# Expert stage of a hybrid trunk layer: TensorE in source order, gathers and scatters in few groups

## The chip, the cores and the metric

One NeuronCore of one Trainium2 chip runs the whole program. The metric is the time of one execution on the device, in microseconds. The kernel is written with a planner (Tile): the program text gives instructions and data dependences; the planner allots buffers, sets semaphores and, by its own simulated time, chooses the order in which each engine issues. All operands are float32 in HBM.

## The reference, cut to what matters

One layer on 512 latent and 256 context tokens of width 2048: modulation, one input projection, two mixers (S5 and DeltaNet), output projection and LayerNorm; then an expert-choice mixture of experts on the 512 latent tokens, gate and a second LayerNorm. The change touches only the mixture and what follows it:

```python
aff = softmax(h @ router_w); gate, idx = top_k(aff.swapaxes(1, 2), cap)   # 16 experts, cap = 64 tokens each
sel = h[idx]                                                              # (16, 64, 2048)
hid = silu(sel @ w1) * (sel @ w3)                                         # w1, w3: 2048 x 1024 for each expert
y = (hid @ w2) * gate                                                     # w2: 1024 x 2048 for each expert
ff = zeros.at[idx].add(y)
x = layer_norm(ALPHA * x + g2 * ff, ln2_g, ln2_b)
```

## The kernel before, in words

The expert stage (lines 1845 to 1876) takes the experts two at a time, eight pairs `pr`. The 64 tokens of one expert fill one half of TensorE's columns, those of the other the other half (`tile_position=(0, 64 * a)`, a = 0, 1). A matmul with f32 operands shows as two records in the profile.

For each pair the work is:

- `gather` (L1444): VectorE writes a one-hot matrix `oh` (L1450); TensorE multiplies the 512 token rows `K.y` (names in the profile: mixed) with it, 16 matmuls or 32 records for each of four groups q (L1458); ScalarE applies the modulation while it copies a group from PSUM to `selT` (L1461). `oh` and `selT` have one buffer each.
- `expert_in` (L1508): eight steps of four loads of 1 MB (`load_in`, the DMA issue is L1477), each step 16 matmuls (32 records, L1522) into four PSUM banks `acc4`. Then `hid` is made (ScalarE L1527, VectorE L1528 and L1529), transposed (L1534) and copied to `hT` (L1535). `slots` (L1492) transposes `oh` into the scatter matrix `G` and fetches the gates `gc`.
- `expert_out` (L1545): two halves of the output columns, four steps each, a step being two loads of 1 MB and 8 matmuls (16 records, L1556). After each half `gated` (L1599) multiplies by gate and `g2r` (L1604), and splits the result in two parts `yp` (L1605, L1606). After steps 1 to 7 and at the end, a function `fill` inserts other work: a gather group of the next pair at even steps, scatter blocks 0 and 1 at steps 6 and 7.
- `scatter_chunk` (L1610): for one block of 512 columns, four times two matmuls (L1616) into a bank of `pp`, and VectorE adds it to `acc` (L1618). Blocks 2 and 3 come during the next pair's `expert_in`.

`merge` interleaves two generators in the text; but the text is only a priority, and the planner may reorder TensorE's instructions as its simulation finds data ready. DMA issues are all on SyncE's queue, in order. The loads go through 13 rotating buffers `ws` of 1 MB (`NWS`) and seven once-used ones `wy` for the first pair; a load waits until TensorE has read what was in its buffer.

PSUM has four banks `mp`, three banks `pp` (gather, scatter, transposes) and one `po`. In SBUF `hid`, `yp` and `ln1g` share two buffers (tag row), `ln1b` and `g2r` share one (tag g2r).

`acc_start` (L1638) makes the residual: rows of ln1 are spread over the partitions by `on_rows` (four transposes to a bank, then a copy by ScalarE, L1634 and L1635), VectorE multiplies (L1649) and GpSimd adds (L1650), eight operations of 128x1024 each; then `g2r` is made by `on_rows`. It is called once, between the first pair's `expert_in` and its `expert_out`. The last pair has its own second product `expert_last` (L1566), which ends in `K.fin` (L1593), and `finish` (L1655) normalises and stores.

Of the kernel before, what the change touches and what calls it, by code (L numbers as in the profile page):

```python
# [11 lines left out]
F32 = mybir.dt.float32  # L12
# [7 lines left out]
MUL, ADD, SUB = ALU.mult, ALU.add, ALU.subtract  # L20
# [6 lines left out]
KT = D // 128  # L27
# [18 lines left out]
def bc(a, shape):  # L46
    return a.to_broadcast(shape)


def mp(K, shape=(128, 4, 128), tag="mp"):  # L50
    return K.ps.tile(list(shape), F32, name=tag, tag=tag, bufs=K.banks[tag])


def pp(K, n=512):
    t = K.ps.tile([128, 512], F32, name="pp", tag="pp", bufs=K.banks["pp"])
    return t[:, :n]
# [796 lines left out]
def merge(*parts):  # L853

    live = [[g, n, 0] for g, n in parts]
    while live:
        e = min(live, key=lambda x: x[2] / x[1])
        e[2] += 1
        try:
            next(e[0])  # L860
        except StopIteration:
            live.remove(e)
# [6 lines left out]
GA = 1  # L869
# [574 lines left out]
def gather(K, pr, ep, S):  # L1444

    nc = K.nc
    V, A, T = nc.vector, nc.scalar, nc.tensor
    oh = ep.tile([128, 4, 2, 64], F32, name="oh")
    for a in range(2):
        V.tensor_tensor(oh[:, :, a], bc(K.iota64[:, None, :], [128, 4, 64]), bc(K.slot[:, :, 2 * pr + a:2 * pr + a + 1], [128, 4, 64]), op=ALU.is_equal)  # L1450
    S.oh = ohf = oh.rearrange("p b a s -> p b (a s)")
    S.selT = ep.tile([128, KT, 128], F32, name="selT")
    for q in range(4):
        pg = pp(K).rearrange("p (a b) -> p a b", a=4)
        for j in range(4):
            k = 4 * q + j
            for b in range(4):
                T.matmul(pg[:, j], K.y[:, k, b], ohf[:, b], start=(b == 0), stop=(b == 3))  # L1458
        for j in range(4):
            k = 4 * q + j  # L1460
            A.activation(S.selT[:, k], pg[:, j], AF.Identity, scale=K.A[:, k:k + 1], bias=K.B[:, k:k + 1])  # L1461
        yield
# [18 lines left out]
def load_in(K, I, pr, k0, w, a, gate=None):  # L1481
    return load(K, [128, 2, FF], ap(I[("exp_w1", "exp_w3")[w]], (2 * pr + a) * D * FF + k0 * 128 * FF, [[FF, 128], [128 * FF, 2], [1, FF]]), gate)
# [9 lines left out]
def slots(K, pr, S):  # L1492

    V, A, T = K.nc.vector, K.nc.scalar, K.nc.tensor
    S.G = K.ep2.tile([128, NL], F32R, name="G")
    pg = pp(K)
    for b in range(4):
        T.transpose(pg[:, 128 * b:128 * b + 128], S.oh[:, b], K.ident)
    A.copy(S.G, pg)
    pg = pp(K, 2)  # L1500
    for b in range(4):
        T.matmul(pg, S.oh[:, b], K.aff[:, b, 2 * pr:2 * pr + 2], start=(b == 0), stop=(b == 3))
    S.gc = K.ep2.tile([128, 1], F32, name="gc", bufs=2)
    for a in range(2):
        V.tensor_copy(S.gc[64 * a:64 * a + 64], pg[64 * a:64 * a + 64, a:a + 1])


def expert_in(K, I, pr, S):  # L1508
    nc = K.nc
    V, A, T = nc.vector, nc.scalar, nc.tensor  # L1510
    acc4 = [mp(K, (128, 512)) for _ in range(4)]
    for k0 in range(0, KT, 2):
        ws = {}
        for w in range(2):
            for a in range(2):
                ws[w, a] = load_in(K, I, pr, k0, w, a)
        for w in range(2):
            for kk in range(2):
                k = k0 + kk
                for c in range(2):  # L1520
                    for a in range(2):
                        T.matmul(acc4[2 * w + c][64 * a:64 * a + 64], S.selT[:, k, 64 * a:64 * a + 64], ws[w, a][:, kk, 512 * c:512 * c + 512],  # L1522
                                 start=(k == 0), stop=(k == KT - 1), tile_position=(0, 64 * a))
        yield
    hid = K.ep2.tile([128, 2, 512], F32, name="hid", tag="row", bufs=2)
    for c in range(2):
        A.activation(hid[:, c], acc4[c], AF.Tanh, scale=0.5)  # L1527
        V.scalar_tensor_tensor(hid[:, c], hid[:, c], 1.0, acc4[c], op0=ADD, op1=MUL)  # L1528
        V.scalar_tensor_tensor(hid[:, c], hid[:, c], 0.5, acc4[2 + c], op0=MUL, op1=MUL)  # L1529
    S.hT = K.ep2.tile([128, 8, 128], F32, name="hT")  # L1530
    for c in range(2):
        pt = pp(K).rearrange("p (a b) -> p a b", a=4)
        for j in range(4):
            T.transpose(pt[:, j], hid[:, c, 128 * j:128 * j + 128], K.ident)  # L1534
        A.copy(S.hT[:, 4 * c:4 * c + 4], pt)  # L1535
    slots(K, pr, S)
    yield


def load_out(K, I, pr, a, f, n, c0, w):  # L1540
# [69 lines left out]
def scatter_chunk(K, S, c, end=False):  # L1610
    s = slice(512 * c, 512 * c + 512)
    t = S.yp.pop(c)
    for b in range(4):
        ps = K.fin[b] if end else pp(K)
        for i in range(2):
            K.nc.tensor.matmul(ps, S.G[:, 128 * b:128 * b + 128], t[:, i], start=not end and i == 0, stop=i == 1)  # L1616
        if not end:
            K.nc.vector.tensor_tensor(K.acc[:, b, s], K.acc[:, b, s], ps, op=ADD)  # L1618
        if K.st2 is not None:
            K.nc.vector.bn_stats(K.st2[:, b, c], ps if end else K.acc[:, b, s])  # L1620


def scatter(K, S):
    for c in (2, 3):
        scatter_chunk(K, S, c)
        yield


def on_rows(K, dst, cols, scale=1.0, n=4):

    for q in range(n):
        pt = pp(K)
        for j in range(4):
            K.nc.tensor.transpose(pt[:, 128 * j:128 * j + 128], bc(cols[:, 4 * q + j:4 * q + j + 1], [128, 128]), K.ident)  # L1634
        K.nc.scalar.activation(dst[:, 512 * q:512 * q + 512], pt, AF.Copy, scale=scale)  # L1635


def acc_start(K, I, pool):  # L1638

    nc = K.nc  # L1640
    K.acc = pool.tile([128, 4, D], F32, name="acc")
    lb = pool.tile([128, D], F32, name="ln1b", tag="g2r")
    on_rows(K, lb, K.cols[:, 112:128], ALPHA)
    for h in range(2):
        lg = pool.tile([128, 8, 128], F32, name="ln1g", tag="row", bufs=2)
        on_rows(K, lg.rearrange("p k c -> p (k c)"), K.cols[:, 96 + 8 * h:104 + 8 * h], ALPHA, 2)
        s = slice(1024 * h, 1024 * h + 1024)
        for b in range(4):
            nc.vector.tensor_tensor(K.acc[:, b, s].rearrange("p (k c) -> p k c", k=8), K.y[:, 8 * h:8 * h + 8, b], lg, op=MUL)  # L1649
            nc.gpsimd.tensor_tensor(K.acc[:, b, s], K.acc[:, b, s], lb[:, s], op=ADD)  # L1650
    K.g2r = pool.tile([128, D], F32, name="g2r", tag="g2r")
    on_rows(K, K.g2r, K.g2[:, :, 0])


def finish(K, I, O, ep, lg, lb):  # L1655
# [22 lines left out]
def hybrid_trunk_kernel(tc, I, O):  # L1678
    nc = tc.nc
    K = Ctx()  # L1680
    K.nc, K.tc = nc, tc
    with ExitStack() as es:
# [24 lines left out]
        right = lambda name: tc.tile_pool(name=name, bufs=1, side="right", reuse_waits="tile")  # L1707
# [125 lines left out]
        with tc.tile_pool(name="p3", bufs=1, reuse_waits="tile") as p3:  # L1833
# [8 lines left out]
            wy = ExitStack()  # L1842
            K.wy = wy.enter_context(right("wy"))
            route(K, plog, p3)
        with tc.tile_pool(name="ep", bufs=1, reuse_waits="tile") as ep, ExitStack() as e2s:
            K.st2 = None
            S = [Ctx() for _ in range(8)]
            first = gather(K, 0, ep, S[0])
            for _ in range(GA):
                next(first)  # L1850
            begun = expert_in(K, I, 0, S[0])
            merge((first, 4 - GA), (itertools.islice(begun, 8), 8))
            wy.close()
            K.ep2 = e2s.enter_context(right("ep2"))
            for _ in begun:
                pass
            acc_start(K, I, K.ep2)
            for pr in range(8):
                S[pr].yp = {}
                if pr:  # L1860
                    merge((expert_in(K, I, pr, S[pr]), 9), (scatter(K, S[pr - 1]), 3))
                if pr < 7:
                    nxt = gather(K, pr + 1, ep, S[pr + 1])

                    def fill(step):
                        if step % 2 == 0:
                            next(nxt, None)
                        if step in (6, 7):
                            scatter_chunk(K, S[pr], step - 6)
                    expert_out(K, I, pr, S[pr], fill)  # L1870
            K.st2 = ep.tile([128, 4, 4, 6], F32, name="st2")
            l2 = K.yh("ln2", F32).rearrange("p (a q) n -> p a (q n)", a=4)
            l2 = [l2[:, i] for i in range(2)]
            for i in range(2):
                on_rows(K, l2[i], K.ln2[:, i])
            expert_last(K, I, 7, S[7])
            finish(K, I, O, ep, *l2)


# [26 lines left out]
```

## Time and profile before

| | us |
|---|---|
| median of 3 runs | 2703.14 (2702.12 to 2708.47) |
| profiled execution | 2703.15 |
| its span | 2701.4 |
| TensorE busy in the span | 2467.7 (91%) |
| VectorE, ScalarE, GpSimd busy | 1300.9, 717.7, 783.6 |
| matmuls of L1522 and L1556 | 468.9 and 298.2 |
| bytes read from HBM | 646.12 MB (258 GB/s over the span) |

The profile is one execution, times in us from the start of the span. PE is TensorE, PEld its weight loads, DVE VectorE, ACT ScalarE, POOL GpSimd, SPq the queue of SyncE that issues the DMAs. A row of a timeline or chain is a run of instructions of one line: start, length, engine, line, operation, out<-in, count, and in brackets the idle time before it with what ended it. "issue" is idle time for which the profile shows no cause. [...] Busy matmul time counts overlapped matmuls once in a sum over an engine.

### The profile page before, as it was taken

The page shows a single profiled execution, that of the slowest core. Times are in us where ns is not written, and L with a number is a line of the kernel's source. Part 1 is how long each engine was busy: PE and PEld are TensorE (multiplying, and loading weights), DVE is VectorE, ACT ScalarE, POOL GpSimd, SP SyncE. Part 2 cuts the span into 40 slices and gives each one's busy share as a digit, 9 for nine tenths or more (in the row PEclk, how much of TensorE's full clock was granted, in tenths as well). Part 3 has the DMA queues.
Part 4 walks back from the last instruction along what each step waited for, and adds up shares of the span by engine and source line. Part 5 has one row for each costly group of instructions (what it writes and reads, how often), then busy time and mean ns, then how long its engine had stood idle before and what let it go on. Part 6 is the DMA issues. An engine that isn't in the chain of part 4 may idle for free. (4 is left out here: it accounts for less than half of the span.)

```text
span 2701.4 us, 41223 instructions
## 1 busy us (share of the span) xinstructions
PE 2467.7 (91%) x16062; PEld 1541.3 (57%) x16062; DVE 1300.9 (48%) x2831; ACT 717.7 (27%) x1611; POOL 783.6 (29%) x747
## 2 busy tenths in 40 slices
PE   7998989899878989899999859999999999999994
PEld 4665778778756766566667724434444444444441
DVE  3362685899577677767877560411111101010106
ACT  2223233534544344443333330201010101010111
POOL 2341275631255464545454410400000000000002
PEclk9998999999988999899999979999999999999997
DMA  9956847766654456777763287998999999999893
GB/s 281 323 176 166 266 148 210 195 163 163 187 158 123 116 174 197 239 224 227 225 194 85 63 319 276 362 382 339 390 384 389 383 390 366 406 366 408 350 406 128
DMA packets 444317, 698.73 MB, mean 259 GB/s; under 512 B 91288, under 2 KB 271001, under 8 KB 443097
## 3 DMA queue, kind: packets, MB, share of 16 engines
q1 hardware_dynamic: 438745, 693.82, 74.6%
q10 hardware_dynamic: 5376, 2.26, 0.4%
q8 instruction: 127, 2.08, 0.3%
q14 instruction: 69, 0.57, 0.1%
HBM read 646.12 MB, written 49.87 MB: 258 GB/s over the span
## 5 line engine op out<-in xcount | busy, mean ns | idle before, releaser
L390 POOL TENSOR_TENSOR wl<-wr,wh 128x512 fp32r<-128x512 f32 (+2 forms) x248 | 335.2, 1354 | 609.3 <-ACT wh L388 577.9
L1522 PE MATMUL mp<-ws,selT 128*64 128x512 f32 x1992 | 468.9, 594 | 0.5 <-ACT selT L1461 0.5
L1522 PEld LDWEIGHTS mp<-ws,selT 128*64 128x64 f32 x1992 | 176.2, 137 | 265.7 <-issue 258.8
L1556 PE MATMUL mp<-ws,hT 128*64 128x512 f32 x896 | 298.2, 603 | 0.0
L1606 POOL TENSOR_TENSOR yp<-ypf,yp 128x512 fp32r<-128x512 f32 x31 | 39.7, 1280 | 875.0 <-ACT yp L1605 875.0
L388 ACT CAST wh<-wr 128x512 fp32r<-128x512 f32 (+2 forms) x249 | 150.5, 605 | 351.3 <-PE pp L397 140.1
L396 PE MATMUL pp<-hi,wh 128*128 128x512 f32 (+1 forms) x528 | 222.0, 420 | 18.4 <-ACT wh L388 18.4
L398 PE MATMUL pp<-hi,wl 128*128 128x512 f32 (+1 forms) x528 | 221.6, 420 | 16.3 <-POOL wl L390 16.3
L397 PE MATMUL pp<-lo,wh 128*128 128x512 f32 (+1 forms) x528 | 217.4, 412 | 0.0
L1528 DVE SCALAR_TENSOR_TENSOR hid<-hid,mp 128x512 f32<-128x512 f32 x16 | 11.0, 688 | 354.9 <-ACT hid L1527 354.1
L1604 DVE SCALAR_TENSOR_TENSOR ypf<-mp,gc,g2r 128x512 f32<-128x512 f32 x32 | 24.0, 751 | 318.5 <-issue 184.9
L1556 PEld LDWEIGHTS mp<-ws,hT 128*64 128x64 f32 x896 | 83.5, 136 | 141.9 <-issue 130.2
L1618 DVE TENSOR_TENSOR acc<-acc,pp 128x512 f32<-128x512 f32 x124 | 79.1, 683 | 162.7 <-PE pp L1616 162.7
L1458 PEld LDWEIGHTS pp<-oh,mixed 128*128 128x128 f32 x1024 | 123.5, 197 | 57.3 <-issue 57.3
L1461 ACT ACTIVATE selT<-pp,colB,colA 128x128 f32<-128x128 f32 x128 | 48.3, 457 | 341.8 <-PE pp L1458 341.8
L1458 PE MATMUL pp<-oh,mixed 128*128 128x128 f32 x1024 | 136.8, 287 | 1.3 <-DVE oh L1450 1.3
L398 PEld LDWEIGHTS pp<-hi,wl 128*128 128x128 f32 (+1 forms) x528 | 102.7, 195 | 49.1 <-POOL wl L390 25.3
L396 PEld LDWEIGHTS pp<-hi,wh 128*128 128x128 f32 (+1 forms) x528 | 104.0, 197 | 37.3 <-ACT wh L388 23.0
L397 PEld LDWEIGHTS pp<-lo,wh 128*128 128x128 f32 (+1 forms) x528 | 104.1, 197 | 18.3 <-issue 4.7
L1527 ACT ACTIVATE hid<-mp 128x512 f32<-128x512 f32 x16 | 9.6, 597 | 381.6 <-PE mp L1522 381.6
L217 PE MATMUL ada<-aw,cT 128*32 128x512 f32 x448 | 100.1, 633 | 11.8 <-DMA aw<-in_ada_w_dram 7.3
L396 PE MATMUL pp<-oph,wh 128*128 128x512 f32 x240 | 98.9, 417 | 6.7 <-DVE Z L666 3.5
(583 smaller groups left out, 4819.2 us busy)
## 6 DMA issues: line engine op xcount, KB each, us to landing
ws<-in_exp_w_dram SPq DMA_DIRECT2D x375, 1024.0 KB
aw<-in_ada_w_dram SPq DMA_DIRECT2D x184, 512.0 KB
wr<-in_w_in_dram SPq DMA_DIRECT2D x157, 256.0 KB
wr<-in_w_out_dram SPq DMA_DIRECT2D x52, 256.0 KB
cl<-CL SPq DMA_DIRECT2D x8, 1024.0 KB
P<-tp SPq DMA_DIRECT2D x32, 256.0 KB
B<-tb SPq DMA_DIRECT2D x32, 256.0 KB
CLo<-cl SPq DMA_DIRECT2D x16, 512.0 KB
```

What stands on the lines that cost most here:

```text
L217: nc.tensor.matmul(pa[32 * j:32 * j + 32], K.cT[:, k], aw[:, kk], start=k < 4, stop=k >= 12, tile_position=(0, 32 * j))
L388: nc.scalar.copy(wh, wr)
L390: (nc.vector if K.nsp % K.sv == 1 else nc.gpsimd).tensor_tensor(wl, wr, wh.bitcast(F32), op=SUB)
L396: T.matmul(out, wh, hi, start=st, stop=False, **kw)
L397: T.matmul(out, wh, lo, start=False, stop=False, **kw)
L398: T.matmul(out, wl, hi, start=False, stop=sp, **kw)
L1458: T.matmul(pg[:, j], K.y[:, k, b], ohf[:, b], start=(b == 0), stop=(b == 3))
L1461: A.activation(S.selT[:, k], pg[:, j], AF.Identity, scale=K.A[:, k:k + 1], bias=K.B[:, k:k + 1])
L1522: T.matmul(acc4[2 * w + c][64 * a:64 * a + 64], S.selT[:, k, 64 * a:64 * a + 64], ws[w, a][:, kk, 512 * c:512 * c + 512], start=(k == 0), ...
L1556: T.matmul(acc[c][64 * a:64 * a + 64], S.hT[:, f0 + f, 64 * a:64 * a + 64], ws[a][:, f, 512 * c:512 * c + 512], start=(f0 + f == 0), stop= ...
L1606: (nc.vector if end else nc.gpsimd).tensor_tensor(t[:, 1], y, t[:, 0].bitcast(F32), op=SUB)
L1618: K.nc.vector.tensor_tensor(K.acc[:, b, s], K.acc[:, b, s], ps, op=ADD)
```

## The change

From the start of the expert stage TensorE issues in the order of the text (`tc.manual_schedule` for this engine alone); the other engines stay with the planner. `merge` is no longer used there. `expert_in` takes a function `fill` for the places between its steps, and its tail becomes `hidden`, which puts one gather group of the next pair ahead of the transposes. The places are now:

- first pair: gather group 0, then groups 1 to 3 after steps 1, 3 and 5 of `expert_in`; `slots` after it; `acc_start` in two pulls after steps 1 and 2 of `expert_out`; the next pair's gather group 0 in `hidden`, group 1 after step 3, and after step 8: scatter block 0, group 2, scatter block 1, group 3;
- later pairs: the same, but scatter 0, group 2, scatter 1, group 3 after step 7; scatter block 2, `slots` and scatter block 3 after step 2 of the next `expert_in`;
- last pair: the rows of ln2 after steps 4 and 6 of `expert_in`, not after the seventh pair's end.

In `acc_start` every second add moves from GpSimd to VectorE.

```diff
-def expert_in(K, I, pr, S):
+def expert_in(K, I, pr, S, fill):
...
-        yield
+        if k0 + 2 < KT:
+            fill(k0 // 2 + 1)
+
+
+def hidden(K, S, fill):
...
+    fill()
     S.hT = K.ep2.tile([128, 8, 128], F32, name="hT")
     for c in range(2):
         pt = pp(K).rearrange("p (a b) -> p a b", a=4)
         for j in range(4):
             T.transpose(pt[:, j], hid[:, c, 128 * j:128 * j + 128], K.ident)
         A.copy(S.hT[:, 4 * c:4 * c + 4], pt)
-    slots(K, pr, S)
-    yield
...
-            nc.gpsimd.tensor_tensor(K.acc[:, b, s], K.acc[:, b, s], lb[:, s], op=ADD)
+            (nc.vector if b % 2 else nc.gpsimd).tensor_tensor(K.acc[:, b, s], K.acc[:, b, s], lb[:, s], op=ADD)
+    yield
     K.g2r = pool.tile([128, D], F32, name="g2r", tag="g2r")
     on_rows(K, K.g2r, K.g2[:, :, 0])
+    yield
...
+            es.enter_context(tc.manual_schedule(engines={mybir.EngineType.PE}))
             K.st2 = None
             S = [Ctx() for _ in range(8)]
-            first = gather(K, 0, ep, S[0])
...
+            l2 = []
+            nxt = gather(K, 0, ep, S[0])
+            next(nxt)
             for pr in range(8):
                 S[pr].yp = {}
...
+                def fill_in(step):
+                    if pr == 0:
+                        if step in (1, 3, 5):
+                            next(nxt)
+                    elif step == 2:
+                        scatter_chunk(K, S[pr - 1], 2)
+                        slots(K, pr, S[pr])
+                        scatter_chunk(K, S[pr - 1], 3)
+                    elif pr == 7 and step in (4, 6):
...
+                        on_rows(K, l2[step // 2 - 2], K.ln2[:, step // 2 - 2])
+
+                expert_in(K, I, pr, S[pr], fill_in)
+                if pr == 0:
+                    wy.close()
+                    K.ep2 = e2s.enter_context(right("ep2"))
+                    slots(K, pr, S[pr])
+                nxt = gather(K, pr + 1, ep, S[pr + 1]) if pr < 7 else iter(())
+                hidden(K, S[pr], lambda: next(nxt, None))
+                if pr == 7:
+                    K.st2 = ep.tile([128, 4, 4, 6], F32, name="st2")
+                    expert_last(K, I, pr, S[pr])
+                    break
+                if pr == 0:
+                    begun = acc_start(K, I, K.ep2)
+
+                def fill_out(step):
+                    if pr == 0 and step in (1, 2):
+                        next(begun)
+                    if step == 3:
+                        next(nxt)
+                    if step == (8 if pr == 0 else 7):
+                        for c in range(2):
+                            scatter_chunk(K, S[pr], c)
+                            next(nxt)
+
+                expert_out(K, I, pr, S[pr], fill_out)
             finish(K, I, O, ep, *l2)
```

## Rows read from the trace of the kernel before

**Rows 1.** The page, the span in 40 slices: what the DMA engines moved.
```profile
GB/s 281 323 176 166 266 148 210 195 163 163 187 158 123 116 174 197 239 224 227 225 194 85 63 319 276 362 382 339 390 384 389 383 390 366 406 366 408 350 406 128
```

**Rows 2.** Windows: us, busy us (instructions) by engine, TensorE clock, DMA share, GB/s.
```profile
1910.00:2010.00 100.00, 99.81 (x439) 45.56 (x435) 10.46 (x18) 8.59 (x19) 2.55 (x2) 1.00 1.03 410
2010.00:2040.00 30.00, 29.35 (x126) 13.18 (x126) 6.55 (x10) 2.75 (x6) 2.56 (x2) 1.00 0.80 306
1903.39:2034.17 130.78, 129.94 (x567) 59.07 (x568) 17.02 (x29) 11.33 (x25) 5.11 (x4) 1.00 0.97 385
```

**Rows 3.** Waits of the DMA queue, 1500 to 2702: us, times, longest.
```profile
SPq L1477 <- PE mp L1522: 406.5, 152, 34.9
```

**Rows 4.** Chain of waits, expert stage: start us, us, what.
```profile
1628.76 20.75 PE mp L1522 x96
1903.39 49.38 PE mp L1522 x224
1955.42 1.86 PE mp L1556 x4
1959.49 3.58 PE mp L1556 x12
```

**Rows 5.** Timeline, weight loads of the second product: start us, us, engine, line.
```profile
1955.35 0.19 PEld L1556 LDWEIGHTS mp<-ws,hT 128*64 128x64 f32 x2
1955.84 0.14 PEld L1556 LDWEIGHTS mp<-ws,hT 128*64 128x64 f32 x1 [0.29 <-issue]
1957.21 2.08 PEld L1458 LDWEIGHTS pp<-oh,mixed 128*128 128x128 f32 x18 [0.81 <-issue]
```

**Rows 6.** Timeline, TensorE: a gather group, then a scatter group.
```profile
1648.48 0.14 PEld L1522 LDWEIGHTS mp<-ws,selT 128*64 128x64 f32 x2 [0.28 <-issue]
1649.44 3.84 PE L1458 MATMUL pp<-oh,mixed 128*128 128x128 f32 x32
1653.20 0.13 PEld L1522 LDWEIGHTS mp<-ws,selT 128*64 128x64 f32 x1
1792.38 1.20 PE L1616 MATMUL pp<-yp,G 128*128 128x512 f32 x4
1793.50 4.50 PE L1522 MATMUL mp<-ws,selT 128*64 128x512 f32 x18
```

**Rows 7.** By line: count, shortest/median/longest ns, first and last start.
```profile
L1649 DVE TENSOR_TENSOR acc<-mixed,ln1g x8: 1217/3375/3377, 1709.6 to 1728.3; 128x1024 f32<-128x1024 f32 x8
L1650 POOL TENSOR_TENSOR acc<-acc,ln1b x8: 2334/3335/3341, 1710.9 to 1733.9; 128x1024 f32<-128x1024 f32 x8
L1674 DVE TENSOR_TENSOR acc<-acc,ln x4: 1209/1210/3253, 2679.7 to 2695.1; 128x1024 f32<-128x1024 f32 x4
```

**Rows 8.** Chain of waits around the start of acc.
```profile
1709.55 1.24 DVE acc L1649
1710.92 20.85 POOL acc L1650 x7
1736.23 0.61 ACT g2r L1635
1736.88 1.11 PE pp L1634 x4
```

**Rows 9.** Timeline, ScalarE: first eviction of the first gather.
```profile
1625.27 1.50 ACT L1461 ACTIVATE selT<-pp,colB,colA 128x128 f32<-128x128 f32 x4 [21.71 <-PE pp L1458]
```

**Rows 10.** Windows: after an idle TensorE, an earlier stage, and the end.
```profile
1735.00:1745.00 10.00, 8.12 (x49) 8.12 (x50) 2.25 (x3) 4.47 (x10) 3.74 (x3) 0.66 1.03 411
2640.00:2645.00 5.00, 5.00 (x18) 2.02 (x17) 3.88 (x7) 0.00 (x0) 0.00 (x0) 1.00 1.03 381
2645.00:2650.00 5.00, 3.44 (x16) 1.13 (x13) 2.69 (x5) 0.62 (x1) 0.43 (x1) 1.00 0.07 26
1000.00:1020.00 20.00, 13.75 (x69) 9.52 (x67) 19.02 (x40) 6.67 (x16) 15.94 (x19) 0.83 0.67 224
```

**Rows 11.** Timeline, VectorE: the last product taken up.
```profile
2663.92 0.75 DVE L1604 SCALAR_TENSOR_TENSOR ypf<-mp,gc,g2r 128x512 f32<-128x512 f32 x1 [6.35 <-PE mp L1586]
```

More of the change, by code (lines that the diff above doesn't have):

```diff
@@ L1505, in slots @@
         V.tensor_copy(S.gc[64 * a:64 * a + 64], pg[64 * a:64 * a + 64, a:a + 1])
-def expert_in(K, I, pr, S):
-    nc = K.nc
-    V, A, T = nc.vector, nc.scalar, nc.tensor
-    acc4 = [mp(K, (128, 512)) for _ in range(4)]
+def expert_in(K, I, pr, S, fill):
+    T = K.nc.tensor
+    S.acc4 = acc4 = [mp(K, (128, 512)) for _ in range(4)]
     for k0 in range(0, KT, 2):
@@ L1523, in expert_in @@
                                  start=(k == 0), stop=(k == KT - 1), tile_position=(0, 64 * a))
-        yield
+        if k0 + 2 < KT:
+            fill(k0 // 2 + 1)
+def hidden(K, S, fill):
+    nc = K.nc
+    V, A, T = nc.vector, nc.scalar, nc.tensor
+    acc4 = S.acc4
     hid = K.ep2.tile([128, 2, 512], F32, name="hid", tag="row", bufs=2)
@@ L1620, in scatter_chunk @@
             K.nc.vector.bn_stats(K.st2[:, b, c], ps if end else K.acc[:, b, s])
[L1623 to L1626, printed above, removed]
 def on_rows(K, dst, cols, scale=1.0, n=4):
@@ L1845, in hybrid_trunk_kernel @@
         with tc.tile_pool(name="ep", bufs=1, reuse_waits="tile") as ep, ExitStack() as e2s:
+            es.enter_context(tc.manual_schedule(engines={mybir.EngineType.PE}))
             K.st2 = None
             S = [Ctx() for _ in range(8)]
-            first = gather(K, 0, ep, S[0])
[L1849 to L1854, printed above, removed]
@@ L1855, in hybrid_trunk_kernel @@
-            for _ in begun:
-                pass
-            acc_start(K, I, K.ep2)
+            l2 = []
+            nxt = gather(K, 0, ep, S[0])
+            next(nxt)
             for pr in range(8):
                 S[pr].yp = {}
[L1860 to L1876, printed above, removed]
+                def fill_in(step):
[7 more added lines that the diff above has]
+                    elif pr == 7 and step in (4, 6):
+                        if not l2:
+                            t = K.yh("ln2", F32).rearrange("p (a q) n -> p a (q n)", a=4)
+                            l2.extend(t[:, i] for i in range(2))
+                        on_rows(K, l2[step // 2 - 2], K.ln2[:, step // 2 - 2])
```

## The prediction

> **What bounds the kernel now.** Read the slices of the span first, for the rate of the transfers [rows 1]. From the 24th slice on (the expert stage, from about 1620 us) most slices move 380 to 410 GB/s, so this stage is near the memory's pace. The stage must bring in 16 experts x 3 matrices x 2048 x 1024 x 4 B = 384 MB (MB is 2^20 B here), 48 for each of the eight pairs of experts: 32 for the first product, 16 for the second. Next the table by windows [rows 2]: over 100 us of a steady stretch 410 GB/s at a DMA share of 1.03, which I take as the ceiling; one whole pair takes 130.78 us at 385 GB/s. At the ceiling its 50.33e6 B take 50.33e6 / 410e3 = 122.8 us. So each pair loses 8 us of transfer, and it loses them in one place (306 GB/s in the 30 us after 2010). TensorE is busy for 129.94 of the 130.78 us at full granted clock. The DMA queue's own waits close the argument: its issues on L1477 stood 406.5 us behind matmuls of L1522 alone [rows 3], that is, behind a buffer that TensorE had not yet read. TensorE sets the period and the transfers follow.
>
> Then ask why TensorE needs 130.8 us, from the chain of waits [rows 4]. A matmul in f32 is two records, and the two experts of a pair fill two halves of the array, so two records can run beside each other. Unbroken, 96 records take 20.75 us: 0.432 us for two. In the second product 4 records take 1.86 us and the next 12 take 3.58, so one step of 16 takes 5.44 us where eight times 0.432 would be 3.46. The timeline of the weight loads says why [rows 5]: loads that come two at a time in an unbroken run come singly here, so one half of the array works while the other stands. The planner's order has taken the experts apart. The last row of that group shows the other price: the load of a full-width group (the gather) starts only 0.81 us after the one before it.
>
> **The change, part by part.** Sums are on the profiled execution (span 2701.4 us, 2703.15 us in all, so 1.75 us lie around the span; the median of the runs is 2703.14).
>
> TensorE's work for one pair afterwards. First product: 128 twos x 0.432 = 55.3 us. Second: 64 x 0.432 = 27.6. A gather of 32 records, with its two changes of shape, takes the time from 1648.48 + 0.43 to 1653.20, 4.3 us [rows 6]; now 4 of these, undivided: 17.2. The scatter: 4 records in 1.12 us with a change of shape [rows 6], 32 records in four blocks, at most 9.0. Hidden part and slots: today 1903.39 + 49.38 = 1952.77 to 1955.35, 2.6 us [rows 4, 5]. One gather now stands ahead of the transposes, so ScalarE must first write four selT pieces (1.50 us, [rows 9]) before it copies hT: plus 1.5. Sum 113.2 us, 17.6 less than now and 9.6 less than the 122.8 of the transfers. The grouped scatter reads banks as fast as VectorE empties them; that could add 2 or 3 us, inside those 9.6. So the steady pair becomes bound by transfers: 122.8 us. The 13 buffers hold 33 us of transfers at 2.56 us each (1048576 / 410e3). The longest run of TensorE that reads no weights (scatter, gather, scatter, gather after step 7 of the second product) is 2 x 4.3 + 2 x 2.2 = 13 us: it is covered, the queue does not run dry.
>
> The first pair is different, and here the new order costs. Its expert_in starts after one gather instead of two: first eviction at 1625.27, start about 1626 [rows 9]. With 55.3 + 3 x 4.3 it ends at 1694.2. Then 2.6 + a gather of 3.8 + about 2.1 (estimate: selT again, and oh, which must be written anew) bring the second product to 1702.7; step 1 ends at 1706.2. Now acc_start is pulled: 8 row groups at 0.61 us of ScalarE each [rows 8]; the first half of ln1g is there at about 1710.9, as it is now (1709.55). Step 2 ends near 1715. The next pull writes g2r, which shares its buffer with ln1b and so waits for the last of the adds into acc. Three banks take three transposed groups; the fourth must wait, and in source order everything behind it on TensorE waits too: steps 3 to 8 of the second product, and through them every buffer that the DMA queue needs.
>
> How long? Today eight multiplies on VectorE and eight adds on GpSimd take 1709.55 to 1736.2 [rows 8]. A multiply takes 1.217 us alone and 3.375 beside GpSimd, an add on GpSimd 2.334 alone and 3.335 beside VectorE, an add on VectorE 1.209 at best [rows 7]: the two engines hardly overlap. Half the adds move. One multiply with one add now takes 20.85 / 7 = 2.98 us, so an add costs 1.76 beside VectorE's 1.217. Taken as one queue the low end is 8 x 1.217 + 4 x 1.209 + 4 x 1.76 = 21.6 us; the high end lets each GpSimd add hold VectorE for its longest time, 4 x 3.335: 27.9. I take 23.5, an add at 2.2, near the low end because alone and together the two nearly add up (1.217 + 2.334 = 3.55 against 3.38). The chain ends at 1734.4, the fourth group at 1736.1. TensorE has then stood since 1716.5, 19 us, and starts at the lower clock: today's shorter stand before 1736.88 [rows 8] left a granted 0.66 over ten microseconds [rows 10], 3 us of work lost. Step 3 ends at 1742.6.
>
> Transfers, counted from 0: 45 to 48 go out with steps 1 and 2 (to 1715) and have landed by 1720. The 49th needs the buffer of step 3: idle 22.5 us. Steps 4 to 8 with one gather release 51 to 60 until 1764; these land until 1776. The group after step 8 ends at 1777.4; the first buffer of the next pair is free at 1780.8, another 5 us idle. From there the queue is never empty: 384 - 61 = 323 MB x 2.56 = 827 us, last landing at 2608.
>
> The end. Today the transfers stop at 2645 [rows 10], since TensorE runs behind, and the last product is taken up at 2663.92 [rows 11], 37.5 us before the end. That tail (last scatter, statistics, output) is not touched, the two ln2 rows only go earlier into slack. After the change TensorE is waiting when the last data land: 1.7 us of matmuls, plus 1.7 for the fin products which now stand in order before them. 2608 + 3.4 + 37.5 = 2648.9; with 1.75 it is **2650.6 us**, 1.9% under the median.
>
> [...]
>
> **The rivals.**
> First, a shorter first pair (14%): the planner orders VectorE and GpSimd so that the wait for g2r hides, or g2r is early. For it: the adds lose half of their GpSimd work. Against: the fourth bank must wait in any order. Without the 22.5 us: 2628.
> Second, TensorE stays the bound (12%): grouped evictions wait on VectorE or ScalarE, and the pair takes 124 to 128 us. expert_in of the second pair ends at 1777.4 + 55.3 + 7 = 1840; six pairs of 126 and some 84 for the end give 2680 + 1.75 = 2682, with 128 it is 2694. For it: four blocks share three banks of pp in each scatter, and nothing may now pass a group that waits. Against: the 9.6 us of slack.
> Third, no change (6%): the emitted order does not keep the experts paired, or grouped waits eat the 17.6 us: 2703.
> [...]
>
> **How the numbers follow.** The forecast has 62% with its own range 2640 to 2668 (adds 21.6 to 27.9 us; the ceiling 403 to 410 GB/s, 323 MB at 0.04 us more is 14). The range of 2627 to 2692 takes in the first rival and most of the second. About 0.3%, 8 us, is what a measurement of this kernel tells from no change: faster holds the forecast, the first and nearly all of the second, 0.87; same the third and a rest, 0.07; slower 0.06.
>
> **What would show it.** Right: L1556 in twos and 16 records in about 3.5 us; L1458 in blocks of 32; DMA share near 1.02 from 1785 to about 2608 with pairs of 123 us; TensorE waiting for ws transfers, some 9 us a pair; SyncE's waits behind L1522 much shorter; one wait of some 19 us at L1634 behind g2r, and a slice or two of slow transfers there; the last transfer about 41 us before the end. Wrong: pairs above 125 us with TensorE busy all through (second), a granted clock under 0.9 in the first products (fourth), no stand near 1720 (first).

## The result, and the profile after

The changed kernel takes 2660.56 us (median of 4 runs, 2653.51 to 2664.77) beside 2704.14 us for the kernel before on the same chip (4 runs, 2702.12 to 2708.47). The ratio is 0.9834, 95% interval [0.981, 0.9859]: 1.7% faster. Forecast were 2650.6 us with a range of 2627 to 2692. The profiled execution took 2664.77 us, span 2663.0.

Line numbers moved by one to nine: L1556 is now L1563, L1616 is L1623, L1586 is L1593, L1604 is L1611, L1634 is L1635, L1649 and L1650 are L1650 and L1651.

The page, the span in 40 slices: busy tenths of TensorE, and what the DMA engines moved.

```profile
PE   7998989889977998799999895789989899898984
...
GB/s 276 322 182 175 267 154 193 203 171 155 183 159 127 122 124 232 204 233 206 232 239 128 42 236 288 292 286 406 409 409 409 409 409 409 409 409 409 409 406 159
```

Where [rows 1] swung between 350 and 408 GB/s, ten slices in a row now stand at 409, TensorE in tenths at 8 or 9. One dip comes before them (292, 286).

The windows give the reason, with columns as in [rows 2] (the clock is the granted one, a mean over the window, with 1.00 for full speed): two whole pairs, from scatter to scatter, and two stretches of the first pair.

```profile
2155.84:2279.38 123.54, 113.27 (x566) 50.74 (x568) 17.04 (x29) 11.23 (x25) 5.08 (x4) 0.99 1.03 409
2279.38:2402.95 123.57, 113.18 (x566) 50.33 (x568) 16.86 (x28) 11.23 (x25) 5.08 (x4) 0.99 1.03 409
1720.00:1737.50 17.50, 0.04 (x1) 0.05 (x1) 16.69 (x10) 0.69 (x2) 9.76 (x3) 0.62 0.34 126
1740.00:1760.00 20.00, 20.00 (x106) 8.91 (x104) 1.50 (x2) 2.74 (x6) 2.54 (x2) 0.97 0.69 258
```

A pair went from 130.78 us [rows 2] to 123.6, and TensorE's share of it from 129.94 to 113.2 busy. The transfers at 409 GB/s now fill the whole pair, so the bound has changed hands. The third row is what it cost: 17.5 us in which TensorE did nothing, the transfers ran dry and VectorE was busy almost throughout.

The chain of waits, one pair: start us, us, what.

```profile
1909.01 7.07 PE mp L1522 x32
...
1916.79 18.64 DMA ws<-in_exp_w_dram
...
1937.26 18.63 DMA ws<-in_exp_w_dram
...
1965.42 7.14 PE mp L1563 x32
...
1973.23 18.48 DMA ws<-in_exp_w_dram
```

In [rows 4] this chain held one piece of 49.38 us of TensorE; now three stretches of transfers, 55.8 us of the pair's 122.6, stand between its pieces. And the second product runs 32 records in 7.14 us, 3.57 for 16, where the same 16 took 1.86 + 3.58.

The page's groups of TensorE, busy us and mean ns, then the idle time ahead of them and what ended most of it:

```profile
L1522 PE MATMUL mp<-ws,selT 128*64 128x512 f32 x1992 | 447.1, 595 | 42.0 <-DMA ws<-in_exp_w_dram 41.2
...
L1563 PE MATMUL mp<-ws,hT 128*64 128x512 f32 x896 | 204.1, 599 | 13.5 <-ACT hT L1544 8.5
```

One record lasts as long as before (599 ns; 603 on the page of before), but the second product is busy for 204.1 us instead of 298.2. That is 94.1 us over seven pairs (the last pair has a line of its own), and nearly all of it lies in pairs 2 to 7: 44.62 us in each before, 29.2 after. The first pair, which the planner had left whole, had little to gain (30.48, then 29.77). The first product fell from 468.9 to 447.1 and the gather from 136.8 to 123.5, about 2 to 3 us each in a steady pair. TensorE as a whole is busy 16.7 us less a pair (129.94 against 113.2; overlapping ends count with both lines in the sums by line). Since a record lasts as long as before, the second product's gain is records that stand beside each other: 16 take 3.57 us in one run where 4 and 12 took 5.44.

Waits of the DMA queue, 1500 us to the end: us, times, longest.

```profile
SPq L1477 <- PE mp L1522: 270.8, 119, 31.0
SPq L1477 <- PE mp L1563: 120.2, 52, 24.0
```

The first stood at 406.5 in [rows 3]; behind L1556 it was 286.8 before. The queue still waits for buffers, as it must with 13 of them, but in a steady pair no longer so long that it runs dry.

The timeline of TensorE shows the three places that matter: waits for transfers, the stand in the first pair, and the end.

```profile
1718.09 1.52 PE L1635 MATMUL pp<-ident,ada 128*128 128x128 f32 x12
1737.46 1.11 PE L1635 MATMUL pp<-ident,ada 128*128 128x128 f32 x4 [17.84 <-ACT g2r L1636]
...
2434.81 3.65 PE L1522 MATMUL mp<-ws,selT 128*64 128x512 f32 x16 [1.48 <-DMA ws<-in_exp_w_dram]
2439.92 3.65 PE L1522 MATMUL mp<-ws,selT 128*64 128x512 f32 x16 [1.46 <-DMA ws<-in_exp_w_dram]
...
2600.32 3.65 PE L1593 MATMUL mp<-ws,hT 128*64 128x512 f32 x14 [1.55 <-DMA ws<-in_exp_w_dram]
2603.90 2.25 PE L1623 MATMUL pp<-yp,G 128*128 128x512 f32 x8
2606.09 3.65 PE L1593 MATMUL mp<-ws,hT 128*64 128x512 f32 x16
...
2617.61 3.50 PE L1600 MATMUL pp<-acc,ident 128*128 128x512 f32 x6
2620.95 1.02 PE L1600 MATMUL po<-acc,ident 128*128 128x512 f32 x2
2621.91 3.65 PE L1593 MATMUL mp<-ws,hT 128*64 128x512 f32 x16
```

Late in a first product each half step (16 records, two loads) waits 1.5 us for its transfers, five times in a pair; with one wait of 0.7 us in the second product that is 8.0 us a pair (2155.84 to 2279.38). After 2600.32 no wait for a transfer is left: the last pair's steps come with 8 records of scatter each, 3.6 + 2.2 us, and TensorE works without a break until 2625.6.

VectorE in the same two places, and one add of GpSimd (four of these, 3.21 to 3.25 us):

```profile
1714.39 15.61 DVE L1650 TENSOR_TENSOR acc<-mixed,ln1g 128x1024 f32<-128x1024 f32 x8 [13.37 <-ACT ln1g L1636]
1729.93 6.76 DVE L1651 TENSOR_TENSOR acc<-acc,ln1b 128x1024 f32<-128x1024 f32 x4
...
2625.68 0.75 DVE L1611 SCALAR_TENSOR_TENSOR ypf<-mp,gc,g2r 128x512 f32<-128x512 f32 x1 [4.54 <-PE mp L1593]
```
```profile
1720.12 3.25 POOL L1651 TENSOR_TENSOR acc<-acc,ln1b 128x1024 f32<-128x1024 f32 x1 [1.16 <-DVE acc L1650]
```

One caution before the profiles are compared: the first gather starts at 1625.76 us in this profile and at 1619.85 in the one of before, though the work ahead of it is the same in both. Over all profiles of this study that start lies between 1616.8 and 1629.5. So what follows uses the **stage time**, the span less the start of the first gather: 2701.4 - 1619.85 = 1081.6 before, 2663.0 - 1625.76 = 1037.2 after, 44.3 us less. The medians differ by 43.6. Each stage time is that of one profile. It holds one thing that no edit of these experiments aims at: the first gather and the first one of the next pair take a time that differs from profile to profile. In the changed kernel they took 5.23 and 3.84 us (granted clock 0.71 and 1.00), in experiment 10 6.73 and 5.47. That is 3.1 us more (all gathers are busy for 126.6 us there, 123.5 in the changed kernel), and it is told below where a reading depends on it.

### The profile page after: what moved, and what is told of

Its sections match the earlier page's. It is cut to its first block, busy times and chain, and to the rows that moved or that the text cites. A ratio compares the mean times of both kernels' runs of the same rounds, so it can differ in the third digit from the quotient of the medians.

```text
span 2663.0 us, 41266 instructions
## 1 busy us (share of the span) xinstructions
PE 2353.2 (88%) x16062; PEld 1486.3 (56%) x16062; DVE 1299.6 (49%) x2835; ACT 716.0 (27%) x1611; POOL 770.3 (29%) x743
## 5 line engine op out<-in xcount | busy, mean ns | idle before, releaser
L1522 PE MATMUL mp<-ws,selT 128*64 128x512 f32 x1992 | 447.1, 595 | 42.0 <-DMA ws<-in_exp_w_dram 41.2
L1522 PEld LDWEIGHTS mp<-ws,selT 128*64 128x64 f32 x1992 | 143.0, 137 | 336.6 <-issue 250.2
L1563 PE MATMUL mp<-ws,hT 128*64 128x512 f32 x896 | 204.1, 599 | 13.5 <-ACT hT L1544 8.5
L1611 DVE SCALAR_TENSOR_TENSOR ypf<-mp,gc,g2r 128x512 f32<-128x512 f32 x32 | 24.0, 751 | 244.0 <-PE mp L1563 177.1
L1563 PEld LDWEIGHTS mp<-ws,hT 128*64 128x64 f32 x896 | 66.9, 138 | 135.0 <-issue 107.9
L398 PEld LDWEIGHTS pp<-hi,wl 128*128 128x128 f32 (+1 forms) x528 | 103.1, 195 | 49.3 <-POOL wl L390 25.6
L1458 PE MATMUL pp<-oh,mixed 128*128 128x128 f32 x1024 | 123.5, 279 | 2.5 <-DVE oh L1450 2.5
L398 PE MATMUL pp<-oph,wl 128*128 128x512 f32 x240 | 98.5, 410 | 0.6 <-POOL wl L390 0.6
```

The costliest lines, as they stand in the source:

```text
L398: T.matmul(out, wl, hi, start=False, stop=sp, **kw)
L1563: T.matmul(acc[c][64 * a:64 * a + 64], S.hT[:, f0 + f, 64 * a:64 * a + 64], ws[a][:, f, 512 * c:512 * c + 512], start=(f0 + f == 0), stop= ...
```

## The experiments

All times are medians; the ratio is to the kernel before on the same chip, and is that of the means, so it need not equal the ratio of the medians.

| kernel | us | ratio, 95% interval | stage time |
|---|---|---|---|
| after | 2660.56 | 0.9834 [0.981, 0.9859] | 1037.2 |
| 1 new text, planner's order | 2681.29 | 0.9908 [0.988, 0.9936] | 1052.4 |
| 2 old text, source order | 2667.2 | 0.9862 [0.9835, 0.9889] | 1044.0 |
| 3 experts one behind the other | 2659.76 | 0.9832 [0.9809, 0.9856] | 1039.6 |
| 4 six matmuls more a pair | 2667.16 | 0.9862 [0.9839, 0.9885] | 1038.5 |
| 5 cut between the experts | 2687.55 | 0.9939 [0.9918, 0.996] | 1065.4 |
| 6 cut between twos | 2666.0 | 0.9858 [0.9835, 0.988] | 1044.3 |
| 7 twenty-six matmuls more | 2731.23 (one run) | | 1108.0 |
| 8 all adds on GpSimd | 2663.36 | 0.9854 [0.9824, 0.9885] | 1041.5 |
| 9 adds early | 2651.04 | 0.9795 [0.9771, 0.982] | 1030.6 |
| 10 fin late | 2658.64 | 0.9822 [0.9798, 0.9846] | 1037.6 |
| 11 both | 2650.51 | 0.9792 [0.9769, 0.9814] | 1024.9 |
| 12 both, adds earlier still | 2642.6 | 0.9783 [0.9761, 0.9806] | 1019.0 |

**1. The new text in the planner's order.** Theory: the order of issue alone carries the gain; rival: the new places of gather and scatter do.

```diff
-            es.enter_context(tc.manual_schedule(engines={mybir.EngineType.PE}))
```

> The changed text, but TensorE's order is left to the planner again. Theory (the gain is TensorE's order: experts side by side and undivided groups): the second product falls apart again, a pair takes about 130 us, and the time is 2690 to 2715. Rival (the gain is the new places in the text, half of the adds on VectorE and the earlier ln2 rows): no more than 2670.

2681.29 us, between the two forecasts: a miss for both numbers. The timeline of TensorE shows what the planner kept:

```profile
1970.94 2.72 PE L1458 MATMUL pp<-oh,mixed 128*128 128x128 f32 x22 [0.16 <-ACT selT L1461]
1973.59 1.93 PE L1563 MATMUL mp<-ws,hT 128*64 128x512 f32 x4
1975.45 1.38 PE L1458 MATMUL pp<-oh,mixed 128*128 128x128 f32 x10
```

It still splits groups and still sets 4 records alone between them, but less often: 18 such pieces of four between 1780 and 2560 us, where the kernel before has 48 (eight in each of pairs 2 to 7) and the changed one none. The second product is busy for 237.0 us, between 298.2 and 204.1. There is no stand near 1720 either: its one wait for g2r is 2.6 us. So the new text alone brings 22.9 us of the 43.6 by the medians (29.2 of 44.3 by stage time). What is left is not the share of the order, as the next experiment shows: each of the two removes pieces of four by itself, and their gains do not add up.

**2. The old text in source order.**

```diff
+            es.enter_context(tc.manual_schedule(engines={mybir.EngineType.PE}))
             K.st2 = None
```

> The text of before, and only TensorE's order set to that of the text. Theory (keeping the two experts side by side is what counts, the grouping adds little): pairs of about 123 us, bound by transfers; but the whole of acc_start with its 26 us of adds now stands in TensorE's order ahead of the second product, so the first pair ends some 7 us later than with the change: 2660 to 2675. Rival (large groups are needed): pairs of 128 us or more and 2690 or above.

As forecast. Source order alone is enough for 37 us, most of the gain: no piece of four is left and the second product is busy for 205.3 us. What it lacks to the full change stands in one row of TensorE:

```profile
1729.63 1.11 PE L1634 MATMUL pp<-ident,ada 128*128 128x128 f32 x4 [25.56 <-ACT g2r L1635]
```

All eight adds on GpSimd, and g2r behind them: a stand of 25.56 us instead of 17.84, with 6.8 us more stage time. The medians, 6.6 apart, have intervals that overlap.

**3. The experts one behind the other.** If TensorE pairs only neighbours in its queue, this must bring the slow steps back.

```diff
-                for c in range(2):
-                    for a in range(2):
+                for a in range(2):
+                    for c in range(2):
```

> The changed kernel with the loops over expert and column block exchanged in the second product, so that two matmuls of one expert follow each other (same work, same groups). Theory (side by side is the mechanism): a step takes about 5.6 us instead of 3.5, TensorE needs about 130 us a pair and is the bound again: 2695 to 2710, the whole gain gone. Rival (groups or transfers decide): pairs stay at 123 to 124 us, and the time at 2655 to 2668.

The theory fell, the rival's number came. The timeline of TensorE, then that of its weight loads (both of this kernel):

```profile
1961.04 10.57 PE L1563 MATMUL mp<-ws,hT 128*64 128x512 f32 x48 [1.20 <-ACT hT L1544]
```
```profile
1962.38 0.14 PEld L1563 LDWEIGHTS mp<-ws,hT 128*64 128x64 f32 x1 [0.28 <-issue]
1962.81 0.19 PEld L1563 LDWEIGHTS mp<-ws,hT 128*64 128x64 f32 x3 [0.29 <-issue]
```

48 records take 10.57 us; in the changed kernel a run of 48 takes 10.52 (at 2459.63). The loads come as one and three instead of two and two, but still every 0.43 us. (Of the 2.4 us by which its stage time is longer, the two gathers named above make 2.3: 5.86 and 5.46 us.) Four records of one expert followed by four of the other overlap all the same. What parts the experts must be something between them.

**4. Six matmuls more in each of six pairs.** They do nothing for the result; they tell whether TensorE still sets the pace.

```diff
+                    if 1 <= pr <= 6 and step == 5:
+                        idle = pp(K)
+                        for _ in range(6):
+                            nc.tensor.matmul(idle, K.ident, K.g2r[:, 0:512], start=True, stop=True)
```

> The changed kernel with six extra full-width matmuls (about 6 us of TensorE, result unused) after step 5 of the first product in pairs 1 to 6. Theory (TensorE has some 9 us of slack a pair, transfers set the pace): within 4 us of the changed kernel, 2656 to 2665. Rival (TensorE still sets the pace): 6 x 6 us more, 2695.

12 records of 5.42 us a pair, 32.5 in all, cost 1.3 us of stage time, where TensorE as the bound would have cost all of it. The median misses the forecast's upper end by 2.2 us; it is 6.6 over that of the changed kernel, with intervals that overlap. The window of 130 us, columns as above:

```profile
2160.00:2290.00 130.00, 122.85 (x604) 55.09 (x602) 16.94 (x28) 11.25 (x25) 5.09 (x4) 1.00 1.03 409
```

TensorE is busier, the rate is the same: the transfers set the pace.

**5 and 6. The cut put back, in two places.** Both cut three of the four gathers of a pair into twelve pieces of eight records and put six of them within steps of the second product. Experiment 5 puts each behind the first expert's first two matmuls, experiment 6 behind four whole twos (a two is one record of each expert, side by side). The order of the experts differs too, as the edits show, but experiment 3 has shown that it costs nothing.

```diff
-                for c in range(2):
-                    for a in range(2):
+                for a in range(2):
+                    for c in range(2):
                         ...
+                    if f == 0 and a == 0:
+                        cut(step)
```
```diff
                 for c in range(2):
                     for a in range(2):
                         ...
+                if f == 0:
+                    cut(step)
```

> The changed kernel with gather groups 1 to 3 cut into twelve pieces of 4 matmuls, one after the first expert's first two matmuls and one at the end of each of steps 1 to 6 of the second product (loops as in the run with the experts apart). Theory formed after that run (what costs is a full-width piece that parts the two experts' matmuls, so that four records run alone): a step takes 5.4 us again, TensorE needs about 128 us a pair: 2685 to 2700. Rival (the order of the experts and small groups cost nothing that the transfers do not hide): 2655 to 2668.

> The same twelve pieces, but the first one of a step stands after four whole twos, so that no expert is left alone; as many changes of shape as in the run with the cut between the experts. Theory (the parting of the experts costs, a change of shape only some 0.5 us each): TensorE needs about 118 us, less than the transfers, 2655 to 2668. Rival (the number of changes of shape is the cost): as slow as the other, 2685 or more.

Both came as forecast. TensorE in experiment 5, and then in 6:

```profile
1985.02 1.16 PE L1458 MATMUL pp<-oh,mixed 128*128 128x128 f32 x8
1986.10 3.65 PE L1565 MATMUL mp<-ws,hT 128*64 128x512 f32 x12
1989.68 1.16 PE L1458 MATMUL pp<-oh,mixed 128*128 128x128 f32 x8
1990.77 1.93 PE L1565 MATMUL mp<-ws,hT 128*64 128x512 f32 x4
```
```profile
1971.62 1.94 PE L1565 MATMUL mp<-ws,hT 128*64 128x512 f32 x8
1973.48 1.16 PE L1458 MATMUL pp<-oh,mixed 128*128 128x128 f32 x8
1974.57 1.94 PE L1565 MATMUL mp<-ws,hT 128*64 128x512 f32 x8
```

The first is the very pattern of [rows 4], 4 records in 1.93 us and 12 in 3.65, and its kernel stands at 403 GB/s with TensorE busy for 128.09 of 130 us; the second runs 8 records in 1.94 and stands at 409 with 122.24. The same number of pieces costs 71.6 us more in the second product (285.9 against 214.3 busy), 1.7 us for each of the 42 cut steps, four records of 0.43. So the place of the cut is what counts. It also accounts for the kernels above: 48 pieces at 1.7 us make 82 of the 94.1 us by which the second product got shorter, and the 20 pieces of experiment 1 (18, and two in the first pair) make 34, where its second product was 32.9 over that of the changed kernel. With a full-width group between one expert's matmuls and the other's, 4 records took 1.93 us on one side of it and 12 took 3.65 on the other, where 16 unbroken take 3.57. With one between twos little is lost: from one piece to the next experiment 6 takes 2.95 us (1971.62 to 1974.57), where 8 records of each kind come to 4 x 0.432 + 3.84 / 4 = 2.69 in unbroken runs. (Of the 7.1 us of stage time by which experiment 6 is over the changed kernel, the two gathers make 2.7: 6.27 and 5.47 us. The small pieces also keep TensorE busy longer, 144.2 us on gathers against 123.5, which is not hidden before 1850 us, where the changed kernel has no wait for a transfer; how much that makes was not followed up.)

**7. Twenty-six matmuls more.** The edit of experiment 4 with 26 in place of 6.

> The changed kernel with 26 extra full-width matmuls (0.90 us each, 23.5 us of TensorE, result unused) after step 5 of the first product in pairs 1 to 6. Theory (slack of some 10 us a pair, then TensorE sets the pace): 13 us more in each of six pairs, 2725 to 2750. Rival (the slack is larger or the wait is elsewhere): under 2700.

```profile
2160.00:2290.00 130.00, 127.78 (x594) 57.59 (x592) 16.27 (x27) 10.63 (x24) 3.81 (x3) 0.99 0.94 370
```

As forecast, TensorE sets the pace again. The stage grew by 70.8 us. The two gathers (6.69 and 5.47 us) make 3.1 of it; the rest is 11.3 in each of six pairs, for 22.6 us of added work (135.5 busy in all): 11.3 us were hidden. This is TensorE's slack in a pair; the windows above gave 123.6 - 113.2 = 10.4.

**8. All adds on GpSimd**, as they were before.

```diff
-            (nc.vector if b % 2 else nc.gpsimd).tensor_tensor(K.acc[:, b, s], K.acc[:, b, s], lb[:, s], op=ADD)
+            nc.gpsimd.tensor_tensor(K.acc[:, b, s], K.acc[:, b, s], lb[:, s], op=ADD)
```

> The changed kernel with all eight adds of acc_start on GpSimd, as before. Theory (the two engines share, an add on GpSimd costs 1.8 to 2.3 and on VectorE 1.2 us): the adds take 26.5 us instead of 22.4, TensorE stands 4 us longer behind g2r, and the time rises by 2 to 5 us. Rival (the VectorE adds are what TensorE waits for): the stand gets shorter.

```profile
1734.25 1.11 PE L1635 MATMUL pp<-ident,ada 128*128 128x128 f32 x4 [22.00 <-ACT g2r L1636]
```

The stand grew by 4.2 us (22.00 against 17.84) and the stage by 4.3, with the two gathers as fast as in the changed kernel (5.26 and 3.84 us): the stand goes into the time one for one. The medians, 2.8 apart, agree within their intervals.

**9. The adds early.** If the stand behind g2r is only a matter of when the adds begin, they can begin under the first product, whose TensorE work doesn't need them. The affine's first pull, and the pool that it writes to, go from behind step 1 of the first pair's second product to behind step 6 of its first.

```diff
+                        if step == 6:
+                            wy.close()
+                            K.ep2 = e2s.enter_context(right("ep2"))
+                            l2.append(acc_start(K, I, K.ep2))
+                            next(l2[0])
...
-                    begun = acc_start(K, I, K.ep2)
+                    begun = l2.pop()
...
-                    if pr == 0 and step in (1, 2):
+                    if pr == 0 and step == 2:
```

> The changed kernel with the first pull of acc_start moved up to after step 6 of the first pair's first product, so that the adds run beside the rest of it and g2r's buffer is free when the second pull comes. Theory (TensorE's stand behind g2r empties the DMA queue, and that is lost for good since transfers set the pace afterwards): the stand goes from 17.8 to under 4 us, transfers do not pause near 1730, 18 to 24 us faster: 2636 to 2645. Rival (the queue's pause is made up later, or another wait takes its place): 2652 or more.

6.6 us of stage time, and 9.5 of the median, where 18 to 24 were expected: a miss. The stand behind g2r is gone, but TensorE stands elsewhere. Its timeline, and VectorE's:

```profile
1715.14 6.07 PE L1458 MATMUL pp<-oh,mixed 128*128 128x128 f32 x32 [10.45 <-DVE oh L1450]
```
```profile
1704.81 6.76 DVE L1651 TENSOR_TENSOR acc<-acc,ln1b 128x1024 f32<-128x1024 f32 x4
1711.49 1.27 DVE L1536 SCALAR_TENSOR_TENSOR hid<-hid,mp 128x512 f32<-128x512 f32 x2
...
1714.23 0.76 DVE L1450 TENSOR_TENSOR oh<-rt 128x256 f32<-128x256 f32 x2
```

On VectorE hid and the next oh stood behind the adds: hid starts at 1711.49 us, as the adds end, oh at 1714.23, and TensorE waited 10.45 us for oh. The wait had changed engines. (This profile's two gathers took 6.70 and 6.07 us, 3.7 more than the changed kernel's; without that it would be 10.3 us of stage time, still a miss.)

**10. fin late**, for the end of the kernel: the products of fin stand two steps later in the last pair, behind the last matmuls on weights.

```diff
-            if step == 2:
+            if step == 4:
```

> The changed kernel with the four fin products of the last pair issued after all matmuls on weights instead of between them. Theory (in source order fin waits for banks that VectorE still reads, and the last matmuls wait behind it): the end is 4 us earlier, 2654 to 2660 and a distance from last landing to end of 45 us instead of 49. Rival (VectorE's statistics are the bound there): no change.

The last product was taken up 6 us after the last transfer instead of 10.2, and the end came 44.5 us after it instead of 47.5, close to the forecast. But it is 2 us of a median, no more than its interval can tell. The stage time shows nothing of it because the two gathers of this profile took 3.1 us more than in the changed kernel (given above), as much as the end gained.

**11. Both edits together.**

> Both edits: acc_start's first pull early and the fin products late. Theory (separate places, so they add up): 22 to 28 us faster than the changed kernel, 2632 to 2641. Rival (one takes the other's place): as the better of the two alone.

A miss: 22 to 28 us were expected, and the median, 2650.51, is that of experiment 9 alone, as the rival had it. The wait behind oh (10.48 us) is still there. The stage time is 12.3 us under that of the changed kernel. With the extra time of the two gathers taken out, experiments 9, 10 and 11 gain 10.3, 2.7 and 13.7 us of stage: the places do add up, as the theory said, but what experiment 9 was to bring was put too high.

**12. Both, and the adds one step earlier.** The first of the lines added in experiment 9 reads `if step == 5`.

> Both edits of the run before (fin at the fifth two of the last pair, the affine of the remaining blocks pulled inside the first pair's first products), the pull one step earlier still. Theory: in the run before, TensorE stood 10.5 us because VectorE did the hidden row's products only behind the adds (their last four ended at 1709.2). One step of the first pair earlier is about 6 to 7 us, so the stand should fall to 2 to 5 us and the time by about 6 us against that run: 2644, at least 2639 and at most 2649, if no other stand takes its place. Rival: the loads of the first pair already come as fast as buffers free, so that the stand only moves and the time stays at 2648 to 2653.

```profile
1703.60 5.15 PE L1458 MATMUL pp<-oh,mixed 128*128 128x128 f32 x32 [3.59 <-DVE oh L1450]
```
```profile
1677.70 15.64 DVE L1650 TENSOR_TENSOR acc<-mixed,ln1g 128x1024 f32<-128x1024 f32 x8 [56.91 <-ACT ln1g L1636]
1693.26 6.77 DVE L1651 TENSOR_TENSOR acc<-acc,ln1b 128x1024 f32<-128x1024 f32 x4
```

As forecast: counted from the start of the stage, the multiplies ahead of the adds begin 5.9 us earlier than in experiment 11 (after 56.8 us instead of 62.6), the stand falls from 10.48 to 3.59 us and the stage by 5.9 more, to 1019.0. The times alone do not tell it from experiment 11, whose interval overlaps. At 2642.6 us this version beats both kernels; its interval [0.9761, 0.9806] lies just under that of the changed kernel, [0.981, 0.9859].

## Why the prediction was right, and where it was off

**The bound, and what TensorE saves: right.** 113.2 us of TensorE work were forecast for a pair, 113.2 and 113.3 were measured. The transfers were to take 122.8 and took 123.6, at 409 GB/s instead of 410. Experiments 4 and 7 show the change of hands by themselves: 5.4 us more of TensorE work a pair are nearly free, 22.6 cost 11.3. That 113.2 was hit to a tenth is luck in part: by line, the two products are busy 57.5 and 29.2 us in the pair from 2155.84 (forecast 55.3 and 27.6), the gathers 15.2 (17.2), the scatter 10.3 (9.0), hidden part and slots 2.8 (4.1, of which 1.5 was to be a wait).

**Why the steps were slow: half right.** The prediction said that the planner's order had taken the experts apart. Experiment 3 shows that the order of the experts' matmuls is not the point: one behind the other, they overlap as well (48 records in 10.57 us against 10.52). Experiments 5 and 6 show what is: the full-width piece between them (4 records beside it in 1.93 us, as long as 8 take between whole twos). The number was right because source order removes these pieces whatever the order within a step.

**The adds and the stand: right.** The chain was to take 23.5 us; it took 1714.39 to 1736.69, 22.3. The stand was to be 19 us and is 17.84, experiments 2 and 8 move it with the adds and the time with it. The granted clock was 0.62 over it and 0.50 from 1726 to 1740, and the 16 records behind it took 5.07 us instead of 3.65. The transfers were to lose 22.5 + 5 us; against 409 GB/s the windows lose 25.6 us from 1720 to 1800 (220 GB/s in the first ten, none in the next ten, then 258, 373 and 373 in stretches of 20). That the last landing came within 2 us of the forecast is luck in part, since against the start of the stage the chain ended 3.6 us earlier than forecast, and at the end the transfers slowed (219 GB/s from 2610 to 2615).

**The end: the step that was mis-sized.** "After the change TensorE is waiting when the last data land", with 1.7 + 1.7 us behind it. In the changed kernel's profile the last data landed near 2615.5 (74 GB/s from 2615 to 2616, nothing after) and the last product was taken up at 2625.68: 10.2 us, not 3.4. TensorE was not waiting. In the last pair a step of 16 records and 8 of scatter takes 3.6 + 2.2 = 5.8 us, while its 2.1 MB take 5.4 at the 387 GB/s that the windows show there; so TensorE fell behind in the last steps, and the fin products stood 4.3 us in order ahead of the last 16 records. Of the 10.2 us, 2.1 are the scatter still ahead, 4.3 fin (1.7 forecast) and 3.8 the 16 records of two loads, where the forecast had those of one (1.7). Experiment 10 takes those away and lands at 44.5 us from the last data. The rest of the tail, 37.3 us from the last product on, was forecast at 37.5.

**The sum.** 2650.6 + 5.9 for the later start of the stage in this profile + 1.6 for a last landing that came later (2615.5 against 2608 + 5.9) + 6.6 for the end (47.5 against 40.9) = 2664.7; the profiled run took 2664.77. The median lies 4.2 lower. The start of the stage and the time of the two gathers can make as much between two profiles, but what they were in the other runs is not known.

**The rivals.** A shorter first pair did not come by itself, but experiments 9, 11 and 12 show that it was there to be had: 2642.6 where that rival, for the whole stand, said 2628. TensorE as the bound is what experiment 5 builds, at 2687.55 (the rival: 2682 to 2694). A granted clock under 0.9 in the first products did not come: it is 0.99 over both pairs above, and 1.00 from 2182 to 2207 us, where TensorE waits 1.5 us for transfers after every 3.65. The 0.83 at 1000 to 1020 us [rows 10] stands beside a wait of another kind: TensorE stood 5.9 us there behind one operation of VectorE (L792). The ceiling taken from [rows 2], 410 GB/s, held: 409 stood for ten slices of 66.6 us.

## What to carry to other kernels

Where matmuls of two experts in halves, as here, and full-width ones share TensorE, put the full-width groups between whole twos, few and large: a small group between one expert's matmuls and the other's cost 1.7 us a step here beside its own time (experiments 5 and 6), and with three of a pair's four gathers in pieces of eight records the gathers were busy for 144.2 us in all, undivided for 123.5. When such time is freed, work out first where the next resource stops the gain; here only 7.2 of 16.7 us a pair reached the clock on the wall. And a long chain is moved with an eye on every engine whose work then stands behind it: the adds left TensorE's way only to stand in VectorE's, and TensorE waited 10.45 us there (experiment 9) where it had stood 17.84.

## What the runs showed of the hardware that was not expected

Records of the two experts overlap even where four of one come ahead of four of the other: 48 records in 10.57 us against 10.52 in turn (experiment 3). With a full-width group between the two experts they do not: 1.93 us for 4 records (experiment 5).

A VectorE add or multiply of 128x1024 f32 took 1.21 us alone and a multiply up to 3.38 beside an add of GpSimd, which took 2.33 alone and 3.34 then [rows 7]. 1.21 and 2.33 make 3.54, so the two engines all but took turns here, and four of eight adds moved to VectorE saved 4.2 us of stand though VectorE had the multiplies to do as well (experiment 8).
